# The start of a two-layer decoder step: one hand-ordered list of steps up to the first Strassen tile, activations split straight from PSUM, first weight block on ScalarE's queue

## Chip, cores and metric

One NeuronCore of a Trainium2 chip runs the whole program in one launch. The metric is device time in microseconds (us) per execution, lower is better; the span of the profile is the part of it from the first to the last recorded instruction. TensorE (PE) multiplies, ScalarE (ACT) and VectorE (DVE) do elementwise work, GpSimd (POOL) small things and accumulating DMAs, SyncE (SP) issues most DMAs.

## What is computed

A decoder step for 512 prompt tokens and 8 sample tokens (520 columns in all), width 1024, feed-forward width 2816, two layers. Only the first feed-forward block matters here:

```python
x = x + 0.5 * _swiglu(_rmsnorm(x, norm_g[l, 0]), ffn_w_gate[l, 0], ffn_w_up[l, 0], ffn_w_down[l, 0])

def _swiglu(x, wg, wu, wd):
    return (jax.nn.silu(x @ wg) * (x @ wu)) @ wd
```

Everything is fp32. The kernel reaches that precision with pairs: each operand is split into a high part that TensorE takes exactly and a low part (the rest), and three products (high by high, low by high, high by low) are added.

## The kernel before

**Layout.** Activations are kept turned: eight tiles `x[k]` of 128 rows (128 of the 1024 channels) by 520 tokens. x arrives with tokens in rows, in eight DMAs of 256 KB (`x_load`, L1029: chunk c of 256 channels, in two halves of tokens, called x0.0, x0.1, x1.0, ... below), and is turned on TensorE by transposes (`turn_x`, L1066). The eight sample rows come as two small tiles `xs` on ScalarE's queue (L1018).

**Gate and up product.** The 2816 hidden channels are worked off in 22 tiles of 128. The first three (`NPL[0]`) are plain: two products (gate, up) of 16 parts in all; a part (`part`, L1105, through `mm`, L530) is one k of one product, three terms by two halves of 260 tokens, six matmuls. A product fills a pair of PSUM banks. The later tiles use a Strassen scheme (`strassen_tile`, L629) of seven products of 12 matmuls, for which sums and differences of the x tiles (`sums`, L666) have to be made and split into pairs first. RMSNorm is applied after the products: the row sums of squares are collected in `acc` and turned into `R` by `rstd_tok`, `root` and `rstd_all` (L492 to L524).

**Weights.** `Weights` (L96) loads chunks of 1 MB through SyncE's queue into three rotating buffers and splits them in items of 128 x 512: `hi` on ScalarE (L221, or L195 in the automatic form), the low part on VectorE (L225 or L196). Six split items fit. Items 0 to 3 are the first tile's: gate and up for k 0 to 3 (w0, w1), gate and up for k 4 to 7 (w2, w3). The first chunk comes in four DMAs of 256 KB, issued between the loads of x (L1034 to L1040).

**Order.** A list of steps (`Steps`, L246) carries for each step an engine, a cost, a due time, what it comes after and what buffers it takes; `order` works the list off on paper, on each engine taking the ready step with the earliest due time, and emits the instructions in that order. Each engine then runs its instructions strictly in that order, waiting on semaphores. Lines L1042 to L1182 are such a list for the first tile: t_k (turn x tile k), c_k (copy it to SBUF), s_k (copy its 8 sample columns, L1075), h_k and e_k (high and low part of the scaled x, L1078 and L1082), p_ko (part k of product o), wh_i and wl_i (weight item i), q_k and a_k (square, sum of squares). Its PSUM is three single banks for turned x, one for small things, two pairs for the products. What follows, two plain tiles, the norm, the sums and the first Strassen tile, is written as ordinary code (`ffn`, L689, with `first_hooks`, L1199) and ordered by the automatic scheduler. `begin` (L789) writes the same stretch (plain tiles, norm with a power on GpSimd, sums, products s0 to s5 of the first Strassen tile) as list steps; later feed-forward blocks use it (the fourth at L2392, the second in a similar list behind L1279), the third and the first use the automatic form.

Of the kernel before, what the change touches and what calls it, by code (L numbers as in the profile page):

```python
# [18 lines left out]
P = 128  # L19
D = 1024  # L20
KT = 8
# [295 lines left out]
def yoco_step(ctx, tc, ins, outs):  # L317
# [53 lines left out]
    def ld(dst, src):  # L371
        return lambda raw: later(nc.sync.dma_start(dst(raw), src))
# [8 lines left out]
    def plan_ffn(l, f):  # L381
# [4 lines left out]
        for n in PARTS:  # L386
            for j in range(t0, t0 + n):
# [4 lines left out]
                        ld(lambda raw, k=k, o=o: rows(raw)[:, o, k[0] : k[1], :], w3[:, k[0] : k[1], c])  # L392
# [349 lines left out]
    def weight_steps(st, first, have, count, due, gate=(), width=lambda i: 4, hold=lambda i: []):  # L742
# [16 lines left out]
        for c in sorted(heads):  # L759
# [29 lines left out]
    def begin(st, fi, n, mov, tmp, tt, first, off, base, need, ready, summed, hidden_list, root_):  # L789
# [100 lines left out]
        for p in range(npl):  # L890
# [121 lines left out]
    with ff_pool() as tmp:  # L1012
# [22 lines left out]
        W.begin(2)  # L1035
        x_load(1)
        x_load(2)
        W.begin(4)
# [3 lines left out]
        with tc.tile_pool(name="st", bufs=1, space=bass.MemoryType.PSUM, reuse_waits="tile") as stp:  # L1042
            st = Steps(dict(t=3, m=1, w=6, sq=4))
            add = st.add
            lows, aheads = {}, {}

            def bank(tag, n):
                cnt[0] += 1
                return stp.tile([P, 512], F32, tag=tag, name=f"{tag}{cnt[0]}", bufs=n)

            def warm():
                o = bank("m", 1)
                for _ in range(7):
                    T.matmul(o[:, :P], ones, ones, start=True, stop=True)
# [1377 lines left out]
```

## Time and profile before

| | |
|---|---|
| three runs | 1646.73, 1647.12, 1650.55 us; median 1647.12 |
| the profiled execution | 1648.36 us; its span 1646.6 us |
| TensorE busy | 1633.9 us, 99% of the span |
| VectorE, ScalarE, GpSimd busy | 1237.8, 878.0, 176.8 us |
| mean granted TensorE clock | 0.997 of full speed |

Times of rows are us from the start of the span. A busy TensorE is one with a matmul in flight; how fast it goes is seen from the distance of matmuls and from the granted clock (1.00 is 2.4 GHz, 0.50 is 1.2 GHz). A bracket such as [0.45 <-DMA raw] says how long the engine had been idle before the row and what ended that. In the chain of waits each piece is the work that the next one waited for.

### The profile page before, as it was taken

The numbers are of one execution on the slowest core, as the hardware profiler recorded it, in microseconds if no ns is written. First come the engines' busy times: TensorE is split into PE (matmuls) and PEld (weight loads), VectorE is DVE, ScalarE is ACT, GpSimd is POOL, SyncE is SP. The second block draws the span as 40 slices with busy tenths as digits, with TensorE's granted clock in tenths as the row PEclk, the third lists the DMA queues.
The fourth block names the chain that finished last, engine by engine and source line by source line (L and its number), as shares of the span: only waits on it lengthen the run. The fifth ranks groups of instructions, "written<-read, shape, count | busy, mean of one in ns | idle before, by whom it ended". The sixth has DMA issues, their size and how long they took to land.

```text
span 1646.6 us, 34515 instructions
## 1 busy us (share of the span) xinstructions
PE 1633.9 (99%) x13814; PEld 1620.3 (98%) x13814; DVE 1237.8 (75%) x2341; ACT 878.0 (53%) x1756; POOL 176.8 (11%) x236
## 2 busy tenths in 40 slices
PE   9999999999999999999999999999999999999998
PEld 9999999999999999999999999999989999999998
DVE  7966865878775874878784885778987785785785
ACT  6643643656652652556562552555875663463464
POOL 1101101001101101100201100100220110110100
PEclk9999999999999999999999999999999999999999
DMA  9546846661655755633766666663132575675641
GB/s 245 135 128 129 180 136 140 163 202 54 151 151 135 169 158 135 154 109 97 159 162 154 130 160 159 126 170 103 34 86 71 116 178 141 138 177 137 140 130 53
DMA packets 317567, 226.28 MB, mean 137 GB/s; under 512 B 9536, under 2 KB 293048, under 8 KB 317366
## 3 DMA queue, kind: packets, MB, share of 16 engines
q1 hardware_dynamic: 290976, 178.24, 38.7%
q0 software_dynamic: 23104, 41.31, 15.8%
q10 hardware_dynamic: 3326, 4.53, 0.9%
q8 instruction: 108, 1.77, 0.5%
q14 instruction: 53, 0.43, 0.1%
HBM read 180.63 MB, written 5.04 MB: 113 GB/s over the span
## 4 chain that ended last, share of the span: by engine, by line
PE 95%; DVE 2%; issue 1%; DMA 1%; ACT 0%; SPq 0%; POOLq 0%; POOL 0%; DVEq 0%; ACTq 0%
PE ps L560 48%; PE ps L534 34%; PE pa L534 5%; PE ps L2212 1%; PE pb L1809 1%; PE pc L1880 1%; PE pc L1865 1%; PE p L534 1%; PE ps L1419 1%; DMA pr<-in_bands_dram 1%; PE ps L1382 1%; DMA raw<-in_ffn_w_gate_dram 0%; DVE wl L225 0%; DVE xl L362 0%; DVE acc L487 0%
## 5 line engine op out<-in xcount | busy, mean ns | idle before, releaser
L195 ACT ACTIVATE wh<-raw 128x512 fp32r<-128x512 f32 (+1 forms) x658 | 397.8, 622 | 483.3 <-PE ps L534 284.1
L196 DVE TENSOR_TENSOR wl<-raw,wh 128x512 fp32r<-128x512 f32 (+1 forms) x658 | 435.2, 677 | 175.7 <-ACT wh L195 171.9
L560 PE MATMUL ps<-tl,wh 128*128 128x260 f32 x1248 | 352.4, 282 | 0.0
L560 PE MATMUL ps<-th,wh 128*128 128x260 f32 x1248 | 352.0, 282 | 0.2 <-ACT wh L195 0.2
L560 PE MATMUL ps<-th,wl 128*128 128x260 f32 x1248 | 350.8, 282 | 0.0
L560 PEld LDWEIGHTS ps<-th,wh 128*128 128x128 f32 x1248 | 234.5, 188 | 0.6 <-ACT wh L195 0.4
L560 PEld LDWEIGHTS ps<-tl,wh 128*128 128x128 f32 x1248 | 234.7, 188 | 0.0
L560 PEld LDWEIGHTS ps<-th,wl 128*128 128x128 f32 x1248 | 234.4, 188 | 0.0
L534 PE MATMUL ps<-hl,wh 128*128 128x260 f32 x1024 | 207.2, 282 | 0.0
L534 PE MATMUL ps<-hh,wh 128*128 128x260 f32 x1024 | 206.6, 283 | 0.0
L534 PE MATMUL ps<-hh,wl 128*128 128x260 f32 x1024 | 205.0, 282 | 0.0
L560 PE MATMUL ps<-xh,wh 128*128 128x260 f32 x696 | 195.0, 282 | 0.6 <-ACT sb L643 0.6
L560 PE MATMUL ps<-xl,wh 128*128 128x260 f32 x696 | 194.9, 282 | 0.0
L560 PE MATMUL ps<-xh,wl 128*128 128x260 f32 x696 | 191.6, 282 | 0.0
L158 POOL DMA_DIRECT2D raw<-raw x78 | 69.3, 888 | 1065.0 <-DVE wl L196 387.2
L534 PEld LDWEIGHTS ps<-hl,wh 128*128 128x128 f32 x1024 | 158.3, 188 | 0.0
L534 PEld LDWEIGHTS ps<-hh,wl 128*128 128x128 f32 x1024 | 157.4, 188 | 0.0
L534 PEld LDWEIGHTS ps<-hh,wh 128*128 128x128 f32 x1024 | 157.2, 188 | 0.0
L732 DVE TENSOR_TENSOR u<-ps,R 128x520 f32<-128x520 f32 x86 | 60.0, 698 | 98.5 <-PE ps L534 98.5
L560 PEld LDWEIGHTS ps<-xh,wh 128*128 128x128 f32 x696 | 130.8, 188 | 0.8 <-ACT sb L643 0.8
L560 PEld LDWEIGHTS ps<-xl,wh 128*128 128x128 f32 x696 | 131.1, 188 | 0.0
L534 PE MATMUL ps<-xl,wh 128*128 128x260 f32 x640 | 130.1, 283 | 0.0
(339 smaller groups left out, 3293.3 us busy)
## 6 DMA issues: line engine op xcount, KB each, us to landing
raw<-in_ffn_w_gate_dram SPq DMA_DIRECT2D x87, 512.0 KB
raw<-in_ffn_w_up_dram SPq DMA_DIRECT2D x87, 512.0 KB
raw<-in_ffn_w_down_dram SPq DMA_DIRECT2D x32, 1024.0 KB
S<-in_ffn_w_up_dram SPq DMA_DIRECT2D x78, 256.0 KB
raw<-raw POOLq DMA_DIRECT2D x78, 256.0 KB, 3.3
S<-raw POOLq DMA_DIRECT2D x78, 256.0 KB, 4.5
raw<-in_ffn_w_down_dram SPq DMA_DIRECT2D x16, 768.0 KB
raw<-in_w_q_dram SPq DMA_DIRECT2D x8, 512.0 KB
```

Source lines behind the costliest of these rows:

```text
L158: G.dma_start(blk(raw, 2, 1), blk(raw, 1, 1), accum_op=ALU.add)
L195: nc.scalar.activation(dh, src, AF.Copy)
L196: nc.vector.tensor_tensor(dl, src, dh.bitcast(F32), op=ALU.subtract)
L534: T.matmul(banks[:, hf, :H], a[:, kk, :], hcols(b, hf), start=(first and i == 0), stop=(last and i == 2),)
L560: T.matmul(bank[:, :H], a[:, kk, :], b, start=(not more and kk == 0 and i == 0), stop=(kk == 3 and i == 2), skip_group_check=more,)
L732: V.tensor_tensor(halves(u), banks[m][:, :, :H], halves(R), op=ALU.mult)
L1382: T.matmul(o, a[:, s], b[:, kk, :], start=(n == 0), stop=(n == 5))
L1419: T.matmul(o, za, b, start=(i == 0), stop=(i == len(lst) - 1))
L1809: T.matmul(o, q_[rows_, qc], k_[rows_, kc_], start=(i == 0), stop=(i == 2))
L1865: T.transpose(pt[:, o : o + P], vals["sm", t, h, bi][:, e, kt * P : (kt + 1) * P], ident)
L1880: T.matmul(po[rows_, bi * P : (bi + 1) * P], vtok[:, max(b - 1, 0) + kt, v0 : v0 + 64], vals["pp", t, h, bi][:, kt * 256 + e * P : kt * 25 ...
L2212: T.matmul(bank, a[:, k % 3, :], b[:, c0:c1], start=(k == 0 and i == 0), stop=(k == 5 and i == 2))
```

## The change

The first list now goes on to product s5 of the first Strassen tile, through `begin`, with GpSimd in the order too. x is turned into pairs of PSUM banks (four pairs in all, shared by turned x, both products, the norm and all later tiles), the 8 sample columns are turned in the same step (a fifth transpose), and h_k and e_k read the turned x in PSUM; the copy c_k to SBUF comes after, in one piece, and s_k is gone. A pair is free again when h_k, e_k and c_k have read it. The first weight block (w0) is issued on ScalarE's queue, ahead of the sample rows; w1 to w3 stay on SyncE's. The landing times that the list assumes are new, and so are due times. The square root of the norm is GpSimd's (L808, in `begin`) in place of the twelve small VectorE operations of `root`.

```diff
-    def ld(dst, src):
-        return lambda raw: later(nc.sync.dma_start(dst(raw), src))
+    def ld(dst, src, eng=nc.sync):
+        return lambda raw: later(eng.dma_start(dst(raw), src))
...
+                            lambda raw, k=k, o=o: rows(raw)[:, o, k[0] : k[1], :], w3[:, k[0] : k[1], c],
+                            nc.scalar if k == (0, 4) and o == 0 else nc.sync,
+                        )
                         for k in cuts
                         for o, w3 in ((0, g3), (1, u3))
                     ]
...
-    def weight_steps(st, first, have, count, due, gate=(), width=lambda i: 4, hold=lambda i: []):
...
+            if c in soon:
+                h = heads[c - 2][0]
+                add(f"wa{c}", "POOL", 2.2, due(h) + 0.1, lambda c=c: W.add_up(c), after=[f"wl{h}"])
+                add(f"wd{c}", f"wd{c}", 9.0, -50.0, after=[f"wa{c}"])
+                continue
...
-    def begin(st, fi, n, mov, tmp, tt, first, off, base, need, ready, summed, hidden_list, root_):
...
-        for p in range(npl):
+        for p in range(done, npl):
...
         later(nc.scalar.dma_start(grow, norm_g.rearrange("l n (k p) -> (l n k) p", p=P)))
+        W.begin(1)
         for i in range(2):
...
         x_load(0)
-        W.begin(2)
+        W.begin(1)
         x_load(1)
         x_load(2)
-        W.begin(4)
+        W.begin(2)
         x_load(3)
         W.load(2)
         mov0, tt, st_ = [], {}, {}
-        with tc.tile_pool(name="st", bufs=1, space=bass.MemoryType.PSUM, reuse_waits="tile") as stp:
-            st = Steps(dict(t=3, m=1, w=6, sq=4))
+        open_banks()
+
+        def first_tiles(hs):
+            np_ = NPL[0]
+            st = Steps(dict(d=4, w=6, sb=4, sa=2, g=2, t=2), False)
...
             def turn_g():
-                st_["m"] = o = bank("m", 1)
-                T.transpose(o[:, :48], grow, ident[:48, :48])
-
-            def turn_s():
-                for i in range(KT):
-                    o = st_["m"][:, 64 + i * NS : 64 + (i + 1) * NS]
-                    T.transpose(o, xs[i // 4][:, (i % 4) * P : (i % 4 + 1) * P], ident[:NS, :NS])
+                T.transpose(st_["m"][:, 1, :48], grow, ident[:48, :48])
+
+            def turn_g2():
...
             def turn_x(k):
-                st_["t", k] = pk = bank("t", 3)
+                st_["t", k] = pk = duo().rearrange("p a b -> p (a b)")[:, :TOK]
...
-
-            def copy_x(k, eng, lo, hi):
-                (S.copy if eng == "ACT" else V.tensor_copy)(x[k][:, lo:hi], st_["t", k][:, lo:hi])
-
-            def copy_s(k):
-                V.tensor_copy(x[k][:, SP:TOK], st_["m"][:, 64 + k * NS : 64 + (k + 1) * NS])
+                T.transpose(pk[:, SP:], xs[k // 4][:, (k % 4) * P : (k % 4 + 1) * P], ident[:NS, :NS])
+
+            def copy_x(k, eng):
+                (S.copy if eng == "ACT" else V.tensor_copy)(x[k], st_["t", k])
 
             def x_hi(k):
                 mov0.append(pair(XX, [P, TOK]))
-                S.activation(mov0[k][0], x[k], AF.Copy, scale=gcol(0, k))
+                S.activation(mov0[k][0], st_["t", k], AF.Copy, scale=gcol(0, k))
 
             def x_lo(k):
                 hi, lo = mov0[k]
-                V.scalar_tensor_tensor(lo, x[k], gcol(0, k), hi.bitcast(F32), op0=ALU.mult, op1=ALU.subtract)
+                V.scalar_tensor_tensor(lo, st_["t", k], gcol(0, k), hi.bitcast(F32), op0=ALU.mult, op1=ALU.subtract)
...
-            def w_hi(i):
-                lows[i], aheads[i] = W.hi()
-
-            def w_lo(i):
-                lows.pop(i)()
-                aheads.pop(i)()
-                if i == 4:
-                    W.add_up(3)
...
-                    st_["p", o] = stp.tile([P, 2, 512], F32, tag="p", name=f"p{o}", bufs=2)
+                    st_["p", o] = duo()
...
-            add("i", "POOL", 1.4, -1)
-            add("warm", "PE", 3.0, -1, warm)
-            add("tab", "ACT", 2.4, -1)
-            add("tg", "PE", 0.15, 0, turn_g, after=["i", "lg"])
-            add("cg", "ACT", 0.25, 0.1, lambda: S.copy(gT[:, :48], st_["m"][:, :48]), after=["tg", "tab"])
-            add("ts", "PE", 0.7, 0.2, turn_s, after=["ls", "i", "tg"])
...
+            for name, until in (
+                ("x0.0", 3.7), ("lg", 3.8), ("x0.1", 4.4), ("w0", 4.8), ("ls", 5.0), ("w1", 5.5), ("x1.0", 6.3), ("x1.1", 7.0),
+                ("x2.0", 7.8), ("x2.1", 8.5), ("w2", 9.3), ("w3", 10.0), ("x3.0", 10.8), ("x3.1", 11.5), ("w7", 14.6), ("w11", 17.6),
+            ):
+                land(name, until)
...
+            add("i", "POOL", 3.5, -1)
+            add("warm", "PE", 4.2, -1, warm, takes=("d",))
+            add("tab", "ACT", 4.0, -1)
+            add("tg", "PE", 0.15, 0, turn_g, after=["i", "lg", "warm"], reads=[("g", "preg0")])
+            add("cg", "ACT", 0.22, 0.1, lambda: S.copy(gT[:, :48], st_["m"][:, 1, :48]), after=["tg", "tab"], reads=[("d", "warm")])
...
+            TILE = T0 + 1.6 + UP * 8
+            add("tg2", "PE", 0.12, TILE - 1, turn_g2, after=["i", "t7"], takes=("d",), reads=[("g", "preg1")])
+            add("cg2", "ACT", 0.2, TILE + 6, lambda: S.copy(gT[:, 48:72], st_["m2"][:, :24]), after=["tg2"], reads=[("d", "tg2")])
...
-                    f"t{k}", "PE", 0.45, d, lambda k=k: turn_x(k),
...
-                pieces = [("ACT", 0, 256, 0.37), ("DVE", 256, SP, 0.42)] if k == 0 else [
-                    ("ACT", 0, SP, 0.58) if k % 2 else ("DVE", 0, SP, 0.69)
-                ]
...
-                add(f"s{k}", "DVE", 0.2, d + 0.6, lambda k=k: copy_s(k), after=["ts"])
-                got = [f"c{k}{e[0]}" for e in pieces] + [f"s{k}"]
-                add(f"h{k}", "ACT", 0.72, d + 1, lambda k=k: x_hi(k), after=got + ["cg"] + ([f"h{k - 1}"] if k else []))
-                add(f"e{k}", "DVE", 0.75, d + 1.5, lambda k=k: x_lo(k), after=[f"h{k}"])
+                    f"t{k}", "PE", 0.55, d - 2.4, lambda k=k: turn_x(k),
+                    after=["i", "ls", "tg"] + [f"x{k // 2}.{c}" for c in range(2)] + ([f"t{k - 1}"] if k else []), takes=("d",),
+                )
+                held = [("d", f"t{k}")]
+                add(
+                    f"h{k}", "ACT", 0.72, d + 0.5, lambda k=k: x_hi(k), after=[f"t{k}", "cg"] + ([f"h{k - 1}"] if k else []), reads=held,
+                )
+                add(f"e{k}", "DVE", 0.75, d + 1.0, lambda k=k: x_lo(k), after=[f"h{k}"], reads=held)
+                eng = ("DVE", "ACT")[k % 2]
+                add(
+                    f"c{k}", eng, 0.65 if eng == "ACT" else 0.7, d + 2.0, lambda k=k, eng=eng: copy_x(k, eng), after=[f"t{k}", "tab"] + ([] if k else ["e0"]), reads=held,
+                )
...
-                        f"p{k}{o}", "PE", 0.73, d + 2.3 + 0.7 * o, lambda k=k, o=o: part(k, o),
-                        after=[f"e{k}", f"wl{w}"] + ([f"p{k - 1}{o}"] if k else []),
-                        reads=[("w", f"wh{w}")] if k % 4 == 3 else [],
+                        f"p0.{k}{o}", "PE", 0.73, d + 1.6 + 0.7 * o, lambda k=k, o=o: part(k, o),
+                        after=[f"e{k}", f"wl{w}"] + ([f"p0.{k - 1}{o}"] if k else []),
+                        takes=() if k else ("d",), reads=[("w", f"wh{w}")] if k % 4 == 3 else [],
                     )
...
-                    f"wh{i}", "ACT", 0.63, d, lambda i=i: w_hi(i),
...
-                add(f"o{o}", "ACT", 0.58, T0 + UP * 9 + o, lambda o=o: copy_out(o), after=[f"p7{o}"])
...
+            add("rg", "DVE", 0.7, TILE + 12, gate, after=["o0", "N.c1"])
...
+            def w_due(i):
+                if i < 8:
+                    return (4.6, 5.4, 10.5, 11.2, 17.5, 19.0, 23.0, 24.0)[i]
+                if i < 4 * np_:
+                    return TILE + 2.9 * (i - 4) - 2.0
+                return TILE + 11.6 * (np_ - 1) + 1.4 * (i - 4 * np_) - 5.0
+
+            def landed(i):
+                return [f"w{i}"] if i < 4 else ["w7"] if i < 8 else ["w11"] if i < 12 else []
+
+            weight_steps(st, 0, 0, 4 * np_ + 6 + 4, w_due, hold=landed, soon=(np_,))
+            begin(
+                st, 0, 0, mov0, tmp, tt, 0, 0, TILE - 11.6, lambda k: [], lambda k: [f"c{k}"], ["a7"], lambda: hs, 14.0, 1
+            )
...
-                engines={mybir.EngineType.PE, mybir.EngineType.DVE, mybir.EngineType.Activation}
+                engines={mybir.EngineType.PE, mybir.EngineType.DVE, mybir.EngineType.Activation, mybir.EngineType.Pool}
...
-        open_banks()
-        W.ng = 4
-        there[0] = False
...
-        def first_hooks():
-            steps = sums(tmp, 0, tt)
-            step = lambda: next(steps, None)
...
-                rstd_tok()
-                step()
...
-            def norm_all():
-                rstd_all()
-                known()
...
-            return [step, norm, two, norm_all, two, step, step]
+            begun(0, 0)
...
-        hs0 = ffn(0, tmp, mov0, first_hooks(), tt, HH, deferred(1, tmp, "g", XX, mov1, TW), pool_prep(), first_tile, stop=6)
+        hs0 = ffn(0, tmp, mov0, [], tt, HH, deferred(1, tmp, "g", XX, mov1, TW), pool_prep(), first_tiles, stop=6)
```

## Rows read from the trace of the kernel before

**Rows 1.** The page, busy time of each engine over the span

```profile
PE 1633.9 (99%) x13814; PEld 1620.3 (98%) x13814; DVE 1237.8 (75%) x2341; ACT 878.0 (53%) x1756; POOL 176.8 (11%) x236
```

**Rows 2.** Chain of waits, start and first Strassen tile: start, us, what, matmuls

```profile
9.74 0.85 PE t L1070 x4
10.60 2.36 PE p L534 x18
...
49.40 5.77 PE ps L560 x48
...
56.39 38.89 PE ps L560 x322
```

**Rows 3.** Timeline of the first 8 us, all engines

```profile
1.76 0.47 SPq L372 DMA_DIRECT2D raw<-in_ffn_w_gate_dram  x1
...
4.68 0.20 ACT L1136 COPY gT<-m 128x48 f32<-128x48 f32 x1 [0.95 <-PE m L1059]
5.06 0.20 PEld L1070 LDWEIGHTS t<-ident,xt 128*128 128x128 f32 x2 [0.29 <-DMA xt<-in_x_prompt_dram]
5.43 0.57 PEld L1064 LDWEIGHTS m<-ident,xs 8*128 8x128 f32 x8 [0.17 <-issue]
...
5.95 0.42 DVE L1073 COPY x<-t 128x256 f32<-128x256 f32 x1 [4.92 <-ACT x L1073]
...
6.36 0.63 ACT L221 ACTIVATE wh<-raw 128x512 fp32r<-128x512 f32 x1 [0.45 <-DMA raw<-in_ffn_w_gate_dram]
...
7.66 0.80 PE L534 MATMUL p<-xh,wh 128*128 128x260 f32 x2 [0.98 <-ACT xh L1080]
```

**Rows 4.** DMA view, bytes moved by 4.3, by 5.4 and by 7.8 us

```profile
DMA packets 737, 0.62 MB, mean 143 GB/s; under 512 B 85, under 2 KB 722, under 8 KB 737
...
DMA packets 1392, 0.88 MB, mean 164 GB/s; under 512 B 257, under 2 KB 1376, under 8 KB 1392
...
DMA packets 2482, 1.67 MB, mean 214 GB/s; under 512 B 337, under 2 KB 2466, under 8 KB 2482
```

**Rows 5.** Windows: stretch, length, PE, PEld, DVE, ACT, POOL, PEclk, DMA share, GB/s

```profile
4.00:5.00 1.00, 0.90 (x5) 0.44 (x4) 0.00 (x0) 0.20 (x1) 0.00 (x0) 1.00 0.80 222
7.00:8.00 1.00, 0.34 (x1) 0.34 (x2) 0.98 (x3) 1.00 (x3) 0.00 (x0) 0.75 1.10 358
10.00:11.00 1.00, 1.00 (x7) 1.00 (x6) 1.00 (x2) 0.00 (x0) 0.00 (x0) 0.55 1.15 289
50.00:55.00 5.00, 5.00 (x43) 4.95 (x42) 5.00 (x10) 3.50 (x7) 0.00 (x0) 1.00 0.00 0
```

**Rows 6.** Chain of waits where the second and third feed-forward begin Strassen

```profile
435.52 2.89 PE ps L560 x24
438.42 41.91 PE ps L560 x348
...
802.85 2.90 PE ps L560 x24
806.86 52.12 PE ps L560 x432
```

**Rows 7.** Lines of x's split (source view): count, duration ns min/median/max

```profile
L1080 ACT ACTIVATE xh<-x,gT x8: 712/724/732, 6.9 to 20.0; 128x520 fp32r<-128x520 f32 x8
...
L1084 DVE SCALAR_TENSOR_TENSOR xl<-x,gT,xh x8: 749/756/761, 7.7 to 20.7; 128x520 fp32r<-128x520 f32 x8
...
L1073 DVE COPY x<-t x4: 425/689/692, 5.9 to 16.8; 128x512 f32<-128x512 f32 x3, 128x256 f32<-128x256 f32 x1
```

**Rows 8.** Sample copies, root's first and last operation, GpSimd's power

```profile
L1076 DVE COPY x<-m x8: 155/156/159, 6.3 to 11.4; 128x8 f32<-128x8 f32 x8
...
31.79 0.15 DVE L506 TENSOR_SCALAR nv<-ps 128x5 f32<-128x5 f32 x1
...
35.00 0.16 DVE L513 SCALAR_TENSOR_TENSOR r_tok<-nt,ny 128x5 f32<-128x5 f32 x1
...
L809 POOL TENSOR_TENSOR r_tok<-nv,minus_half x2: 1247/1655/2063, 409.4 to 1286.3; 128x5 f32<-128x5 f32 x2
```

More of the change, by code (lines that the diff above doesn't have):

```diff
@@ L740, in ffn, with weight_steps @@
         return hs
-    def weight_steps(st, first, have, count, due, gate=(), width=lambda i: 4, hold=lambda i: []):
+    def weight_steps(st, first, have, count, due, gate=(), width=lambda i: 4, hold=lambda i: [], soon=()):
         add = st.add
@@ L787, in weight_steps, with begin @@
             add(f"wl{i}", "DVE", 0.14 * n + 0.13, due(i), lambda i=i: w_lo(i), after=[f"wh{i}"] + ([f"wl{i - 1}"] if i else []))
-    def begin(st, fi, n, mov, tmp, tt, first, off, base, need, ready, summed, hidden_list, root_):
+    def begin(st, fi, n, mov, tmp, tt, first, off, base, need, ready, summed, hidden_list, root_, done=0):
         add, vals = st.add, {}
@@ L1112, in copy_out @@
                 S.copy(halves(z), st_["p", o][:, :, :H])
-            def land(name, cost):
-                add(name, "DMA", cost, len(st.steps) - 1000)
-            land("l", 2.4)
-            land("lg", 0.1)
-            for c in range(2):
-                land(f"x0.{c}", 0.87)
-            land("ls", 0.1)
-            for o in range(2):
-                land(f"w{o}", 0.87)
-            for c in range(2, 6):
-                land(f"x{c // 2}.{c % 2}", 0.87)
-            for o in range(2, 4):
-                land(f"w{o}", 0.87)
@@ new lines, in silu, with times, land @@
+            def silu():
+                g = st_["o", 0]
+                S.activation(g, g, AF.Silu)
+            def times():
+                g, t = (st_["o", o] for o in range(2))
+                V.scalar_tensor_tensor(g, t, -1.0, g, op0=ALU.mult, op1=ALU.mult)
+            at_ = [0.0]
+            def land(name, until):
+                add(name, "DMA", until - at_[0], len(st.steps) - 1000)
+                at_[0] = until
+            for name, until in (
[3 more added lines that the diff above has]
+                land(name, until)
@@ L1163, in yoco_step @@
                     )
                 late = d + 9
-                add(f"q{k}", "ACT", 0.63, late, lambda k=k: x_square(k), after=got + [f"h{min(k + 3, 7)}"], takes=("sq",))
+                add(f"q{k}", "ACT", 0.63, late, lambda k=k: x_square(k), after=[f"c{k}", f"h{min(k + 4, 7)}"] + ([f"q{k - 1}"] if k else []), takes=("sb",))
                 add(
                     f"a{k}", "DVE", 0.69, late + 0.5, lambda k=k: x_sum(k),
-                    after=[f"q{k}"] + ([f"a{k - 1}"] if k else []), reads=[("sq", f"q{k}")],
+                    after=[f"q{k}"] + ([f"a{k - 1}"] if k else []), reads=[("sb", f"q{k}")],
@@ new lines, in first_tiles @@
+            add("rg", "DVE", 0.7, TILE + 12, gate, after=["o0", "N.c1"])
+            add("rs", "ACT", 0.65, TILE + 12.3, silu, after=["rg"])
+            add("rm", "DVE", 0.7, TILE + 12.6, times, after=["rs", "o1"], reads=[("t", "o1")])
+            add("Hh0", "ACT", 0.65, TILE + 14, lambda: hidden(st_["o", 0], hs, 0), after=["rm"])
+            add("Hl0", "DVE", 0.7, TILE + 14.5, lambda: hidden_lo(st_["o", 0], hs[0]), after=["Hh0"], reads=[("g", "o0")])
+            def w_due(i):
[4 more added lines that the diff above has]
+                return TILE + 11.6 * (np_ - 1) + 1.4 * (i - 4 * np_) - 5.0
@@ L1181, in yoco_step @@
             ):
                 st.emit()
-        open_banks()
-        W.ng = 4
-        there[0] = False
-        def first_tile(hs):
-            g, t = (st_["o", o] for o in range(2))
-            def rest():
-                V.tensor_tensor(g, g, R, op=ALU.mult)
-                S.activation(g, g, AF.Silu)
-                V.scalar_tensor_tensor(g, t, -1.0, g, op0=ALU.mult, op1=ALU.mult)
-                hidden(g, hs)
-            copied.append(rest)
-            return 1
-        def first_hooks():
-            steps = sums(tmp, 0, tt)
-            step = lambda: next(steps, None)
-            def norm():
-                pg = ps()
-                T.transpose(pg[:, :24], grow2, ident[:24, :24])
-                S.copy(gT[:, 48:72], pg[:, :24])
-                rstd_tok()
-                step()
-            def norm_all():
-                rstd_all()
-                known()
-            def two():
-                step()
-                step()
-            return [step, norm, two, norm_all, two, step, step]
+            begun(0, 0)
@@ L1220, in yoco_step @@
+            return np_ + 1
         prep = {}
```

35 lines of the change are left out of this document (13 added, 22 removed).

## Prediction, made before the change was run

> **What bounds the kernel now.** The page comes first: TensorE is busy 1633.9 of 1646.6 us [rows 1], so 12.7 us of idle in the whole program are all that an order can win, apart from work done at half clock. The chain of waits says where the start loses. Products begin at 7.66 us, after 0.98 us of idle that the high part of x ended [rows 3]; the first part of the first product and the transposes of the third x tile are over at 10.60 [rows 2]. From there TensorE is the chain without a break until the first Strassen tile, which runs four products from 49.40 to 55.17 (49.40 + 5.77) and goes on at 56.39: 1.22 us lost [rows 2]. VectorE is busy in all of the five us before that [rows 5]. The granted clock is 1.00 in the us from 4, 0.75 in the us from 7 and 0.55 in the us from 10 [rows 5]: it fell to 1.2 GHz at about 7.5, when TensorE was idle, and was back at 2.4 GHz at about 10.9. So the change can win at three places: when products start, how long they run slow, and the 1.22 us.
>
> **Start: x, and a new wait.** Before, high part h_0 stood behind two things on ScalarE: the copy of x and the split of w0, which began at 6.36 after waiting 0.45 us for its DMA [rows 3]. The change takes the copies out of the way and lets h_0 read PSUM. But it also changes TensorE's order. Work its list off with its own figures: second half of x1 landed at 7.0 (so t_2 is ready at 7.1), the pair of banks free (t_0, t_1 and t_2 hold three of four), and the first part p_00 ready only at about 7.6, after e_0. So t_2 is emitted ahead of p_00; before it came after it. TensorE then waits for x1 with the whole product stream queued behind it. When does x1 land? By bytes: x0 is 0.52 MB and the small loads 0.09; 0.62 MB were moved at 4.3 us and TensorE's wait for the second half of x0 ended at 5.06. With w0 it is 0.87 MB, moved at 5.4, and ScalarE's wait for w0 ended at 6.36 [rows 3, 4]. So landing follows the last byte by 0.75 to 1.0 us. x0, w0, w1, x1 and the small loads are 1.66 MB, moved at 7.8 [rows 4]: x1 lands at 8.55 to 8.8, I take 8.65, not 7.0. Then t_2's last two transposes at the slow clock (0.43, half of the 0.85 of [rows 2]), the sample transpose (0.57 / 8 = 0.07 [rows 3], 0.14 slow), and p_00 at half speed: 18 matmuls in 2.36 [rows 2] are 0.13 each with a slow first stretch, four full-speed products of 12 in 5.77 are 0.12 each; six at half clock 1.44. That ends at 10.66, against 10.60 for the same work before: **+0.06**. Here goes the gain of the earlier split: h_0 and e_0 are done by about 8 (x0, w0 and the samples behind it land by 6.4, then 0.72 and 0.76 [rows 7]), and what is late next is x1. Bounds: if x1 lands as the list says, p_00 is over at 8.8, and the rest of the slow stretch costs 1.05: 0.9 earlier than now. If the clock comes back 2 us later because TensorE is idle from 6.7 to 7.9, it costs 1.0 more.
>
> The Trainium skill, DMA: Bandwidth & Descriptors, section Issuing engines are not separate DMA queues, speaks against w0 on ScalarE's queue: transfers from several engines share the same DMA engines, and only issue time is saved. The trace has a DMA share of 0.80 at 222 GB/s from 4 to 5 us and 1.10 at 358 from 7 to 8 [rows 5], so there is a hole of some 0.1 MB that a second queue might fill; by that x1 would land 0.25 us sooner, by the page not at all. I take the bytes as they flowed, and leave the 0.25 to the early bound.
>
> **Issues moved.** w0 leaves SyncE's queue (0.47 us of issue) and goes ahead of xs and the activation table on ScalarE. ScalarE had been idle 0.95 us before its first use, the copy of gT, which waited for TensorE [rows 3]; that cover is twice the cost. If it were gone, 0.5 us would show only in h_0, which has the slack until x1. SyncE's later loads go up by one issue.
>
> **Sample columns.** The eight transposes (0.57 together) ran in TensorE's idle time before the first product; now five of them, of t_3 to t_7, lie in the stream: 5 x 0.07 = **+0.35**. The eight copies s_k leave VectorE, 8 x 0.16 [rows 8].
>
> **Norm.** Twelve small VectorE operations between 31.79 and 35.16 [rows 8] go, about 2 us of VectorE; GpSimd's power takes 1.25 to 2.06. TensorE's share is the same. If the sums come as now, the power starts at 31.94 and ends by 34.0, 1.2 before root ends now, at which the products did not stop. On GpSimd it is queued behind the accumulating DMAs of chunk 3 (wa3 is now early in the list), which wait for that chunk; the 1.2 us are the cover. Cost nothing; with the cover gone, R comes late, the gate tiles hold pairs of banks, and TensorE would wait in the third tile.
>
> **First Strassen tile.** The same stretch stands three more times in the program; two of them are shown. In list form there is no gap: 435.52 + 2.89 = 438.41, next at 438.42. In automatic form 802.85 + 2.90 = 805.75, next at 806.86: 1.11 lost [rows 6]. So the form goes with the loss, and VectorE, which was full before it, is relieved of some 3 us (8 x 0.16 and about 2). I take the whole gap: **-1.22**; bounds -1.22 and 0.
>
> **Sum.** 0.06 + 0.35 - 1.22 = -0.81 us. Against the profiled execution, 1648.36, that is 1647.6; against the median, 1647.12, which I forecast, **1646.3 us**. The two differ by 1.24, more than the sum; a measurement of this kernel tells about 0.3% (4.9 us) from no change.
>
> **Rivals.**
> *Early start.* x1 lands near 7, as the list assumes. For it: the hole in the DMA share. Against it: 1.66 MB at 7.8. Then -0.9 + 0.35 - 1.22 = -1.8, 1645.3; if besides the clock never falls, p_00 is over at 8.1 at full speed, 2.5 earlier, and with the five sample transposes and the gap the sum is -3.4, 1643.7.
>
> *The gap stays.* The split of weights into six buffers sets the pace, not VectorE, and the first Strassen tile waits as before or its successor does. For it: ScalarE's splits ended the waits there. Against: the list form elsewhere. Then +0.41, 1647.5.
>
> *Pairs held too long, slower.* Each t_k holds a pair until three readers are through, and only two pairs rotate once the products have theirs. Now three single banks had one reader each. The readers do not overlap: when both engines copied halves of one bank, VectorE's copy began at 5.95, when ScalarE's had ended [rows 3]. The Trainium skill, PSUM — Partial Sum Buffer, section PSUM bank collisions raise a hardware error, says that any two engines on one bank must be kept apart, reads too; the row agrees. A hold is 0.5 (transposes), 0.72, 0.76 and 0.69 [rows 7], 2.67 us, and TensorE needs 1.94 per tile (12 matmuls of 0.12 and 0.5), so it decides from a hold of 3.88. Two foreign operations, as long as 0.72 and 0.76, ahead of the readers on each engine make 5.63, 0.88 per tile too much, for six tiles 5.3: 1651.6; three make 7.11, 9.7 us, 1656.0; middle 1653.8. For it: ScalarE has splits, copies and squares queued between. Against it: they come later by due time.
>
> *The automatic rest shifts.* What follows the list is ordered anew; a new stall is of the size of the 1.11 at 805.75, either way.
>
> **Chances.** Forecast 0.50, early start 0.23, gap stays 0.12, pairs held 0.08, automatic rest 0.07. Low end 1643.6: the early start with the clock kept. High end 1649.3: the forecast with the late clock (+1.0), the gap kept (+1.22), and a run as much above its median as the profiled one was (some 1). Left out are the held pairs and the far ends, under 2 in 10. Faster by over 0.3% (below 1642.2) needs the far early end and a lucky rest, 0.05; slower (above 1652.1) needs held pairs in their upper half or a stall of another kind, 0.06; within, 0.89.
>
> **What the profile would show.** Right: TensorE idle before t_2 with the DMA of x as releaser, t_2's end near 9.2, a fall of the clock about 7.5, the first tile's end 0 to 1 us later than now, no gap at the first Strassen product's successors. Wrong: products before 7.5, TensorE waiting for a copy of x in the first tile (held pairs), a wait for ScalarE's split near 55, or a difference of over 2 us that arises after 60 us.

## The result and the profile after

The changed kernel takes **1650.76 us** (median of 22 runs, 1648.09 to 1653.47); 22 runs of the kernel before beside it took 1648.28 (1646.73 to 1650.55). The ratio is **1.0016** [1.0011, 1.0022]: 2.6 us slower, below the 0.3% that the prediction called distinguishable, but clear of 1 with this many runs, outside the stated range and of the other sign. The forecast was 4.5 us lower; 1.2 of that is its base, a median of three runs (1647.12). The profiled execution took 1650.75 us, its span is 1649.0, 2.4 more than before.

The page, busy time of each engine over the span of the changed kernel:

```profile
PE 1636.5 (99%) x13814; PEld 1621.7 (98%) x13814; DVE 1235.5 (75%) x2322; ACT 876.5 (53%) x1755; POOL 180.6 (11%) x237
```

It answers to [rows 1]: TensorE does as many instructions, 2.6 us longer. Idle time is about what it was (12.5 us for 12.7), so what was lost lies mostly within TensorE's busy time. The chain of waits of the changed kernel, start and first Strassen tile (start, us, what, matmuls; L1075 turns a block of x, L1076 the samples):

```profile
1.24 5.48 DMA xt<-in_x_prompt_dram
...
6.77 0.69 PE ps L1075 x2
...
10.15 2.90 PE ps L537 x12
13.05 0.46 PE ps L1075 x4
13.51 0.15 PE ps L1076
13.66 1.64 PE ps L537 x12
15.30 0.44 PE ps L1075 x4
15.74 0.15 PE ps L1076
...
22.56 4.50 PE ps L537 x36
27.07 0.17 PE ps L1069
...
52.72 16.31 PE ps L563 x134
...
69.04 28.75 PE ps L563 x238
97.79 0.48 PE ps L537 x4
```

The same chain before, behind the pieces of [rows 2]:

```profile
12.96 0.87 PE t L1070 x8
13.84 1.44 PE p L534 x12
...
16.59 7.20 PE p L534 x60
...
95.28 0.48 PE ps L534 x4
```

Cut at four points that both kernels pass, this places the difference as far as 98 us:

| point reached | before | after | lost in the stretch |
|---|---|---|---|
| five x tiles turned, 24 product matmuls done | 13.84 | 15.89 | +2.05 |
| first tile done (96 matmuls) | 23.79 | 27.07 | +1.23 |
| first Strassen product | 49.40 | 52.72 | +0.04 |
| a chain row some four Strassen tiles on (L534 x4, L537 x4) | 95.28 | 97.79 | -0.81 |
| end of the span | 1646.6 | 1649.0 | -0.11 |

The gap of 1.22 at the first Strassen tile is gone; of it 0.81 arrives at the fourth point. The rest was not placed: the list has 372 matmuls in that stretch for 370 before, 0.24 at 0.12 each. The losses up to there are all at the start: 2.05 until the fifth tile, and 1.23 while t_5 to t_7 are turned in the stream.

The -0.11 of the last stretch is small only because larger differences cancel in it. In the chains of waits of before and then of the changed kernel, two places read:

```profile
375.56 10.00 PE ps L1382 x84
...
1212.29 1.46 PE pb L1809 x12
```

```profile
378.37 11.57 PE ps L1364 x84
...
1216.12 0.90 PE pb L1791 x12
```

Both are stretches of low clock in one profile and not in the other. The changed kernel's granted clock was 0.55 from 378 to 380 and 0.60 from 380 to 382, which cost 1.57; that of the kernel before was 0.50 from 1213 to 1215, and what it ran from 1212.29 to 1216.11, 3.82, takes the changed kernel 2.29, a cost of 1.53. The group of 84 took 10.0 us in six of the fourteen profiles of this document and 11.4 to 11.6 in eight, among these run 2, in which only w0 was moved. So one pair of profiles can't tell a difference of this size behind the start; the ratios of many runs can.

The second loss is visible on TensorE's weight loads. Timeline of the changed kernel, engine PEld:

```profile
13.44 0.13 PEld L1076 LDWEIGHTS ps<-ident,xs 8*128 8x128 f32 x1 [0.17 <-issue]
13.59 0.30 PEld L537 LDWEIGHTS ps<-xh,wh 128*128 128x128 f32 x2
...
15.03 0.47 PEld L1075 LDWEIGHTS ps<-ident,xt 128*128 128x128 f32 x4
15.67 0.13 PEld L1076 LDWEIGHTS ps<-ident,xs 8*128 8x128 f32 x1 [0.17 <-issue]
```

Loads otherwise run ahead of the matmuls before them: the one at 15.03 begins before the product at 14.90 is through. The load for an 8-row sample transpose starts only 0.17 after the last load ended (0.33 in the slow stretch at 7.4 to 9.9), and the product's load behind it follows only when it is done. The source view of the line adds it up:

```profile
L1076 PEld LDWEIGHTS ps<-ident,xs x8: 133/134/178, 7.4 to 22.3; 8*128 8x128 f32 x8
...
  issue: 1.8, 8
```

Eight times, 1.8 us. The same bracket stands in [rows 3], at 5.43, once for eight transposes in a row. The few columns of the result are not what does it: in the same profile two matmuls of 8 columns (L825, timeline and source view), but with 128 rows in their load, stand in the stream with no idle time ahead of it.

```profile
37.07 0.30 PEld L825 LDWEIGHTS ps<-ident,r_tok 128*128 128x128 f32 x2
...
L825 PE MATMUL ps<-ident,r_tok x6: 175/216/256, 37.2 to 1291.7; 128*128 128x8 f32 x6
```

### The profile page after: what moved, and what is told of

It reads as the page before. It is cut to its first block, busy times and chain, and to the rows that moved or that the text cites. A ratio compares the mean times of both kernels' runs of the same rounds, so it can differ in the third digit from the quotient of the medians.

```text
span 1649.0 us, 34502 instructions
## 1 busy us (share of the span) xinstructions
PE 1636.5 (99%) x13814; PEld 1621.7 (98%) x13814; DVE 1235.5 (75%) x2322; ACT 876.5 (53%) x1755; POOL 180.6 (11%) x237
## 4 chain that ended last, share of the span: by engine, by line
PE 94%; DVE 2%; DMA 1%; issue 1%; ACT 1%; POOLq 0%; POOL 0%; SPq 0%; DVEq 0%; ACTq 0%
PE ps L563 47%; PE ps L537 35%; PE pa L537 5%; PE ps L2194 1%; PE pb L1791 1%; PE pc L1862 1%; PE pc L1847 1%; PE ps L1401 1%; DMA pr<-in_bands_dram 1%; PE ps L1364 1%; DMA xt<-in_x_prompt_dram 0%; PE ps L1075 0%; DMA pr<-in_pool_w_dram 0%; DVE xl L362 0%; DVE sm L1810 0%
## 5 line engine op out<-in xcount | busy, mean ns | idle before, releaser
L195 ACT ACTIVATE wh<-raw 128x512 fp32r<-128x512 f32 (+1 forms) x646 | 389.9, 621 | 471.4 <-PE ps L537 276.0
L196 DVE TENSOR_TENSOR wl<-raw,wh 128x512 fp32r<-128x512 f32 (+1 forms) x646 | 426.6, 677 | 173.2 <-ACT wh L195 169.5
L537 PE MATMUL ps<-hl,wh 128*128 128x260 f32 x1024 | 207.1, 282 | 0.0
L537 PE MATMUL ps<-hh,wh 128*128 128x260 f32 x1024 | 206.7, 283 | 0.0
L537 PE MATMUL ps<-hh,wl 128*128 128x260 f32 x1024 | 205.0, 282 | 0.0
L563 PE MATMUL ps<-xh,wh 128*128 128x260 f32 x696 | 195.3, 283 | 0.0
L563 PE MATMUL ps<-xl,wh 128*128 128x260 f32 x696 | 194.9, 282 | 0.0
L563 PE MATMUL ps<-xh,wl 128*128 128x260 f32 x696 | 191.9, 282 | 0.0
L537 PEld LDWEIGHTS ps<-hl,wh 128*128 128x128 f32 x1024 | 158.2, 188 | 0.0
L537 PEld LDWEIGHTS ps<-hh,wl 128*128 128x128 f32 x1024 | 157.3, 188 | 0.0
L537 PEld LDWEIGHTS ps<-hh,wh 128*128 128x128 f32 x1024 | 157.2, 188 | 0.0
L537 PE MATMUL ps<-xh,wh 128*128 128x260 f32 x672 | 137.4, 286 | 0.0
L537 PE MATMUL ps<-xl,wh 128*128 128x260 f32 x672 | 136.9, 284 | 0.0
L537 PE MATMUL ps<-xh,wl 128*128 128x260 f32 x672 | 135.5, 283 | 0.0
```

The costliest lines, as they stand in the source:

```text
L195: nc.scalar.activation(dh, src, AF.Copy)
L196: nc.vector.tensor_tensor(dl, src, dh.bitcast(F32), op=ALU.subtract)
L537: T.matmul(banks[:, hf, :H], a[:, kk, :], hcols(b, hf), start=(first and i == 0), stop=(last and i == 2),)
L563: T.matmul(bank[:, :H], a[:, kk, :], b, start=(not more and kk == 0 and i == 0), stop=(kk == 3 and i == 2), skip_group_check=more,)
```

## The experiments

The theories after the first profile: **S**, the sample transposes in the stream cost more than their length; **L**, w0 on ScalarE's queue delays x0; **O**, the list's order (t_2 ahead of the first product) holds the products back; **X**, only the samples behind w0 on that queue are late; **W**, weights further on take back what the start gains. Each run's kernel does the whole computation. Ratios are to the kernel before on the same chip; traces are of one execution each.

### 1. w0 back on SyncE's queue

```diff
-                            nc.scalar if k == (0, 4) and o == 0 else nc.sync,
+                            nc.sync,
...
         later(nc.scalar.dma_start(grow, norm_g.rearrange("l n (k p) -> (l n k) p", p=P)))
-        W.begin(1)
...
         x_load(0)
-        W.begin(1)
+        W.begin(2)
```

> The changed kernel with w0 back on SyncE's queue, behind x0; the list with its orders stays. Theory L (w0 on ScalarE's queue shares the DMA engines with x0 and makes its second half land at 6.73 instead of 5.05): x0 lands near 5.05 again; t_2 then waits for x1, which lands near 8.65, so the first product starts near 9.3 instead of 10.08, 0.8 us earlier, and the kernel is 0.8 us faster than the changed one (about 1.7 us slower than the kernel before). Theory S (the eight sample transposes inside the stream cost the time, about 0.35 us each): first product earlier, but the five later ones still cost 1.75 in the first tile, so 1.5 us or more of the 2.5 stay. If L were all of it, the kernel would come down by the whole 2.5.

Measured: 1651.07 us, 1.0007 [0.9997, 1.0017]. x0 was on time, but t_2 now waited for x1. TensorE in the timeline of this run:

```profile
8.15 0.44 PE L1074 MATMUL ps<-ident,xt 128*128 128x128 f32 x2 [1.18 <-DMA xt<-in_x_prompt_dram]
...
8.90 0.44 PE L1074 MATMUL ps<-ident,xt 128*128 128x128 f32 x2 [0.32 <-DMA xt<-in_x_prompt_dram]
...
9.43 0.51 PE L537 MATMUL ps<-xh,wh 128*128 128x260 f32 x2
```

That is the wait that the prediction worked out (x1 at 8.55 to 8.8). The first Strassen product is at 52.25: only 0.47 of the 3.32 came back in this profile, so theory L explains little of it.

### 2. The kernel before with w0 on ScalarE's queue

```diff
+                            nc.scalar if k == (0, 4) and o == 0 else nc.sync,
...
+        W.begin(1)
         for i in range(2):
             later(nc.scalar.dma_start(xs[i], x_sample[:, 0, i * 512 : (i + 1) * 512]))
```

> The kernel before with w0 on ScalarE's queue ahead of the sample rows, nothing else. Theory L: the second half of x0 lands near 6.7, the first product moves from 7.66 to about 9.2, the kernel gets 1 to 1.5 us slower. Theory S alone: w0 lands a little earlier (6.18 against 6.36), x is late but the split of w0 was what the first product waited for, so no change (within 0.5 us).

Measured: 1650.0 us, 1.0006 [0.9996, 1.0016]. The chain of waits of this run:

```profile
2.46 4.85 DMA xs<-in_x_sample_dram
...
8.85 2.03 PE p L537 x6
...
51.84 5.77 PE ps L563 x48
```

x0 was on time (all four of its transposes ran from 4.75), so it was not x0 that was delayed. Two loads of 16 KB behind 256 KB on one queue took 4.85 us; the first product came at 8.85 instead of 7.66, Strassen at 51.84 instead of 49.40. Of these 2.44, 1.36 is slow clock: 18 matmuls take 3.72 here for 2.36 in [rows 2], at a granted clock of 0.50 from 9 to 15. In this order, where everything waits for the samples, the queue costs in this profile; the ratio's interval still holds 1.

### 3. Sample transposes of 128 rows

The sample tiles get 128 rows, 120 of them zero, so that the fifth transpose has the shape of the other four.

```diff
-        xs = [big.tile([NS, 512], F32, tag=t, name="xs") for t in HH]
+        xs = [big.tile([P, 512], F32, tag=t, name="xs") for t in HH]
+        for z in xs:
+            V.memset(z, 0.0)
...
-                T.transpose(pk[:, SP:], xs[k // 4][:, (k % 4) * P : (k % 4 + 1) * P], ident[:NS, :NS])
+                T.transpose(pk[:, SP : SP + P], xs[k // 4][:, (k % 4) * P : (k % 4 + 1) * P], ident)
```

> The changed kernel with the sample rows laid in tiles of 128 rows (the rest zero), so that their transposes have the shape of the others, 128 x 128; nothing else. Theory S (the 8-row transpose makes TensorE wait 0.17 us before it and about as much after it): each one costs 0.11 instead of 0.35, no idle time in front of it, the first tile shrinks by 5 x 0.24 = 1.2 us, and 0.5 to 0.9 more in the slow stretch: 1.2 to 2.0 us faster than the changed kernel. Theory L alone, or a cost of switching between transposes and products whatever their shape: no change, or 0.04 x 8 = 0.3 us slower.

Measured: 1648.43 us, 0.9999 [0.9990, 1.0007]. The chain of waits of this run (L1079 is the sample transpose):

```profile
14.76 0.44 PE ps L1078 x4
15.20 0.11 PE ps L1079
15.31 1.45 PE ps L537 x12
...
21.28 4.31 PE ps L537 x36
```

Twelve product matmuls take 1.45 where they took 1.64, 36 take 4.31 for 4.50, and the transpose is 0.11 for 0.15; weights now load ahead, with no idle time at full clock. Per tile 0.23 of chain is saved. Theory S holds: a transpose of sixteen times the rows is the cheaper one.

### 4. w0 on SyncE's queue, and landing times of the kernel before

```diff
-                ("x0.0", 3.7), ("lg", 3.8), ("x0.1", 4.4), ("w0", 4.8), ("ls", 5.0), ("w1", 5.5), ("x1.0", 6.3), ("x1.1", 7.0),
+                ("lg", 4.2), ("x0.0", 4.4), ("ls", 4.9), ("x0.1", 5.0), ("w0", 6.3), ("w1", 7.2), ("x1.0", 8.0), ("x1.1", 8.7),
```

(The later entries likewise; beside the edit of run 1.) The list then puts the first part of the first product ahead of t_2.

> The changed kernel with w0 on SyncE's queue and with landing times in the list as the trace of the kernel before shows them (x0 5.0, w0 6.3, w1 7.2, x1 8.7, ...), by which the first part of the first product comes ahead of t_2. Theory L with the order: first product near 7.3, 2.7 us earlier than in the changed kernel, of which some goes at the slow clock; 1.5 to 2 us faster than the changed kernel, 0.5 to 1 slower than the kernel before for the samples in the stream. Theory S alone: 0 to 0.5 us faster than the changed kernel.

Measured: 1650.23 us, 1.0006 [0.9995, 1.0017], so in time no better than run 1, although Strassen began at 50.02, 2.2 earlier, and TensorE ran at full speed from 5.8 on. The chain of waits of this run says what ended last after that:

```profile
50.02 14.87 PE ps L563 x122
...
69.99 7.64 DMA raw<-in_ffn_w_up_dram
...
78.75 8.61 DMA S<-raw
...
96.36 0.53 PE ps L537 x4
```

From 65 to 93 the chain is not TensorE but weights: a load, an accumulating DMA of 8.61, splits on ScalarE and VectorE. Of 2.70 us gained on the changed kernel at 50, 1.43 are left at the last row (96.36 for 97.79).

### 5. The changed kernel once more

No edit.

> The changed kernel itself once more, on the chip of the three that follow. Both theories: 2 to 3 us slower than the kernel before; x0's second half lands at 6.5 to 6.9, the first product starts at 9.8 to 10.3. If the end of the slow stretch at 13.2 was an accident of that one profile, it ends elsewhere here and the first tile's end moves by half of that.

Measured: 1651.83 us, 1.0020 [1.0012, 1.0029]. The timeline of this run:

```profile
5.61 0.63 ACT L221 ACTIVATE wh<-raw 128x512 fp32r<-128x512 f32 x1 [0.70 <-DMA raw<-in_ffn_w_gate_dram]
...
5.83 0.18 PEld L1076 LDWEIGHTS ps<-ident,xs 8*128 8x128 f32 x1 [0.51 <-DMA xs<-in_x_sample_dram]
...
8.00 1.50 PE L1075 MATMUL ps<-ident,xt 128*128 128x128 f32 x4 [0.65 <-DMA xt<-in_x_prompt_dram]
```

x0 was there at 4.6, so its late half in the first profile (6.77) was that execution's; no other profile with w0 on ScalarE's queue (runs 2, 3, 6, 10, 11) has it. Here w0 did come earlier, 5.61 for 6.36 [rows 3], and its low part was done at 6.95, but the products were queued behind t_2 and x1: the first at 9.62, Strassen at 52.68, as late as in the first profile. The slow stretch ended near 13.5, for 13.2 there, so it was no accident of that one profile.

### 6. Samples ahead of w0 on ScalarE's queue

```diff
-        W.begin(1)
         for i in range(2):
             later(nc.scalar.dma_start(xs[i], x_sample[:, 0, i * 512 : (i + 1) * 512]))
+        W.begin(1)
```

> The changed kernel with the sample rows issued ahead of w0 on ScalarE's queue (w0 goes out about 0.9 us later). Theory L as first stated (w0 takes its share from x0): x0's second half still lands after 6, at 6.2 to 6.7, first product at 9.5 to 10.2, within 0.5 us of the changed kernel. Theory X (what is late is the sample rows, behind 256 KB of w0 on their own queue; in the kernel before with w0 moved, TensorE waited for them until 7.3): the rows are there by 5, the first tile's transposes end 0.3 to 0.6 us earlier only if x0 is not the later one.

Measured: 1653.91 us, 1.0026 [1.0017, 1.0035]: the slowest of all. w0 fell back instead, and x1 with it. Timeline of this run:

```profile
8.63 0.63 ACT L221 ACTIVATE wh<-raw 128x512 fp32r<-128x512 f32 x1 [3.82 <-DMA raw<-in_ffn_w_gate_dram]
...
8.88 1.41 PE L1075 MATMUL ps<-ident,xt 128*128 128x128 f32 x4 [2.65 <-DMA xt<-in_x_prompt_dram]
```

The samples did come early, as theory X would have it (their first transpose, at 5.27, waited for no load; in run 5 it waited until 5.83). It won nothing: what was late then was w0 and x1.

### 7 and 8. Runs 3 and 4 together, twice

The edits of runs 3 and 4 in one kernel, measured twice.

> All three start costs undone in the changed kernel: w0 on SyncE's queue, true landing times, sample transposes of 128 rows. Theories L and S together: first product near 7.4, the first Strassen product at 48.7 to 49.2 (50.02 without the wide transposes), no gap behind it; if nothing else limits, 1.5 us faster than the kernel before. Theory W (a chain that the start does not change, weights loaded, summed by DMA and split, ends last in the tiles after the first Strassen tile, as TensorE's late stretch between 65 and 93 us with the true landing times suggests): the end of the first eight tiles stays near 96, and the kernel is level with the kernel before, within 0.7 us.

> The kernel of the run with all three costs of the start undone (first weights on SyncE's queue, landing times and order of the kernel before, 128-row sample transposes), unchanged, for a second measurement. If the three costs are what made the change slower and the closed gap is a real gain, the ratio to the kernel before is below 1 again, 0.9985 to 0.9995 (0.8 to 2.5 us faster), first product by 7.8, no gap after the first Strassen products. If the first measurement was chance, 1.0000 or above.

Measured: 1647.29 us, 0.9991 [0.9983, 1.0000], and 1647.09 us, 0.9993 [0.9984, 1.0002]. The chain of waits of the first of the two:

```profile
49.16 16.34 PE ps L563 x134
...
94.44 0.50 PE ps L537 x4
```

No gap, and the last row at 94.44 (95.07 in the second) for 95.28 before. The ratios put them 1.3 us below the kernel before on average, about what the gap alone would give (1.22). Each interval reaches 1, so the gain over the kernel before is likely, not certain; that over the changed kernel (0.9992 for 1.0016 to 1.0020) is clear.

### 9. Runs 1 and 3 together

w0 on SyncE's queue and 128-row sample transposes, the list's own order.

> The changed kernel with the first weights back on SyncE's queue and with 128-row sample transposes, but with its own landing times and order (third x tile turned ahead of the first product). If queue and sample transposes add up as they measured alone (0.0010 and 0.0018 of 1.0017), this comes out at 0.9988 to 0.9995 of the kernel before, and the order of the list is worth nothing. If the wait for the second x chunk with all products behind it is itself a cost of about 1 us, it comes out near 0.9997 to 1.0003, above the run with the order of the kernel before by 0.0006.

Measured: 1649.69 us, 1.0002 [0.9993, 1.0011]; the first product at 9.25, Strassen at 51.19, against 49.16 and 49.94 with the order of runs 7 and 8. Windows of this run (columns as in [rows 5]) show what the late start costs:

```profile
7.00:8.00 1.00, 0.00 (x0) 0.00 (x0) 0.24 (x1) 0.90 (x2) 0.00 (x0) 1.00 1.09 365
...
12.00:13.00 1.00, 1.00 (x7) 1.00 (x6) 0.87 (x2) 0.00 (x0) 0.00 (x0) 0.50 1.05 338
```

TensorE stands idle through the us from 7, and is still at 1.2 GHz in the us from 12; in the kernel before it was back at 2.4 at about 10.9. With the order of the kernel before eighteen matmuls took 2.17 from 10.57 in run 7 and 2.16 from 11.35 in run 8, 0.12 each, which is full speed; in run 8 the granted clock was 0.50 from 8 to 10 and 0.52 in the us from 10.

### 10 and 11. Only the landing times changed

The changed kernel with w0 still on ScalarE's queue and later landing times in the list ("w0" 6.1, "x1.1" 9.0), once with 8-row and once with 128-row sample transposes.

> The changed kernel, first weights on ScalarE's queue and 8-row sample transposes kept; only the landing times that the list assumes are later, so that the first product's first part stands ahead of the third x tile. If the order (all products behind a transpose that waits for the second x chunk) is what the start loses, the first Strassen product moves from 52.7 to about 50.5 and the ratio from 1.0018 to 1.0005 to 1.0010; if the queue is what counts, products still wait for x or the sample rows, Strassen stays near 52 and the ratio near 1.0015.

> The same with 128-row sample transposes: all of the change but its order and its 8-row transposes. If the queue costs nothing of its own, this is as fast as the run with the first weights on SyncE (0.9985 to 0.9997, first Strassen product near 49.5) or faster by the earlier split of the first weights (5.6 against 7.1); if the queue costs 1 us of its own, 0.9997 to 1.0003, Strassen near 50.5 to 51.

Measured: 1651.09 us, 1.0011 [1.0002, 1.0020], and 1649.9 us, 0.9999 [0.9990, 1.0008]. These landing times didn't do what they were meant to: the list still put t_2 first (in run 10 the first product is at 9.29, Strassen at 52.18; in run 11 at 8.90 and 50.02), so order and queue were not told apart this way. As a pair they tell the sample transposes' cost again, 0.0012.

### 12. The old start, a second list for the gap alone

The first list is that of the kernel before; a second one, through `begin`, orders the two plain tiles, the norm and the first Strassen tile.

```diff
+        def first_tiles(hs):
+            np_ = NPL[0]
+            st = Steps(dict(d=4, w=6, sb=4, sa=2, g=2, t=2), False)
...
+            weight_steps(st, 0, 8, 4 * np_ + 6 + 4, w_due)
...
+            begin(st, 0, 0, mov0, tmp, tt, 0, 0, -11.6, lambda k: [], lambda k: [], ["all"], lambda: hs, 14.0, 1)
```

> The start of the kernel before, list and PSUM unchanged, and then a second list by begin for the two plain tiles, the norm and the first Strassen tile, as in the changed kernel (undoes the start, keeps the rest of the change). Theories L and S: first product at 7.7, first tile's end at 23.8 as before, the norm's root on GpSimd, first Strassen product at 49.4, and no gap: 1.2 us faster than the kernel before. Theory W: the gap at 55 is gone but the same 1.2 us come back as a wait before 100: within 0.4 us of the kernel before.

Measured: 1650.98 us, 1.0005 [0.9995, 1.0015], a miss: it was to show the gap's worth alone and does not. The chain of waits of this run:

```profile
24.69 0.60 ACT t L1112
...
55.55 0.65 ACT wh L221
...
56.96 9.11 PE ps L560 x72
```

The seam between the lists waits for a copy out of PSUM (0.65), and the first Strassen tile for a weight split (1.69 with what stands ahead of it), which I put down to the due times of my list: the gap moved rather than went. Its first product also came late, at 8.54, because w0's split could begin only at 7.24 in this execution (6.36 before, with the same start).

## Why the prediction was wrong

**Taken together.** With nothing else changed, 128-row instead of 8-row sample transposes lower the ratio in four pairs: from 1.0016 or 1.0020 to 0.9999 (run 3), 1.0007 to 1.0002 (runs 1, 9), 1.0006 to 0.9992 (runs 4, 7 and 8), 1.0011 to 0.9999 (runs 10, 11). The mean is 0.0012 to 0.0013, 2.1 us. Each ratio's interval reaches 0.0005 to 0.0011 to either side, so that only the first pair and perhaps the third are clear of noise by themselves; the mean of four, by an estimate from these intervals, is good to some 1 us. Queue and order of the kernel before, put back together, lower the ratio by 0.0012 with 8-row transposes (1.0018 to 1.0006) and by 0.0007 with 128-row ones (0.9999 to 0.9992): about 1.6 us, less certain, though in the traces the first Strassen product moves with it (52.7 to 50.0, and 51.2 to 49.2 and 49.9). What is left with both undone, -1.3, I take for the gap, which the traces of runs 7 and 8 no longer have; run 12, meant to show it alone, did not. 2.1 + 1.6 - 1.3 = +2.4, for 2.6 and 3.3 measured; the parts come from the same ratios as the whole, so that they add up proves little.

**Sample columns, +0.35: the step that failed.** I took the length of eight transposes in a row, divided by eight. That row's own bracket [rows 3] had the price: 0.17 of idle ahead of the group. Spread over the stream it is paid at each transpose (0.15 of chain in all), and again by the product behind it: 12 matmuls take 1.64 for 1.45. That is 0.34 each, 1.7 for the five in the stream, five times the term; the 1.23 of the table is three transposes and four such products. In time, padding all eight to 128 rows won about 2.1 us. The Trainium skill, TensorEngine Tiling (Array Packing), section Key Properties, says that a change of tiling mode drains TensorE; the rows agree with a drain at each change of row count (1.8 us of idle in eight), though no run here shows which mode the 8-row transpose runs in. The Trainium skill, TensorE: Matmul & The Clock Gate, section Step-by-step: what each phase is for, says that the row count doesn't matter for a load's time. The load alone agrees, 133 ns with 8 rows and 139 at the least with 128 (run 3); what stands around it does not.

**Start, +0.06: the second step that failed.** Its mechanism was right: t_2 ahead of p_00, TensorE waiting for x1 with the products behind it, x1 at 8.8 to 9.0 (runs 1, 5, 9), and the earlier w0 (run 5) worth nothing. Only in the first profile was it x0's second half, at 6.77, that TensorE waited for. The first product began at 9.62 in run 5, for 9.22 by the prediction's working (8.65 + 0.43 + 0.14). The size was not right: 2.05 until the fifth tile, of which the sample transposes of t_3 and t_4 and the product between them are 0.49, so the start's own is near 1.6. I let the clock come back at 10.9 as before and kept "2 us later, 1.0 more" as a bound. That bound was the case: in the changed kernel the first twelve matmuls take 2.90 for 1.44 at full clock, 1.46 more, and pairs stand 0.43 apart until 12.85. But the reason that I gave for it, TensorE idle from 6.7 to 7.9, was not the one in the first profile. There the clock was low before the wait, though the granted clock reads 1.00 (see the last section); two loads of the first transposes, before and after, from the timelines:

```profile
4.57 0.20 PEld L1070 LDWEIGHTS t<-ident,xt 128*128 128x128 f32 x2
...
4.60 0.29 PEld L1075 LDWEIGHTS ps<-ident,xt 128*128 128x128 f32 x2
```

0.29 is what the next two take at 6.76 too, and the matmul pairs 0.43 apart follow. In run 1 the clock was back for the transposes of 8.15 (0.20 a pair) and low again from 10 to 13 (0.50), after the us from 7 without work. What lowers it at 4.6 was not tried. The runs put the order and the queue together at 1.6 us; run 2 shows the queue delaying the samples, run 9 the order delaying the products, and by how much each counts alone in the changed kernel stays open: undone singly the queue is worth 0.0011 with 8-row transposes and nothing (0.9999 to 1.0002) with 128-row ones.

**Issues moved, at nothing.** ScalarE's cover held: its idle time before the copy of gT shrank from 0.95 to 0.48 and was not used up. The samples behind w0, by the prediction landed by 6.4, let TensorE go on at 5.8 in run 5, but only at 7.35 in run 2.

**First Strassen tile, -1.22: right in what it does.** No gap in any run of the one list (1, 3 to 11); in the first profile 0.81 of it was left at 98 us, and in time runs 7 and 8 are 1.3 faster than before. Theory W is what can eat it: in runs 1, 4, 5, 6, 11 and 12 weights ended last between 70 and 96, not in the others. Where they did, the slowest accumulating DMA there took 7.9 to 8.6, in the others 5.2 to 8.0; 5.9 in the first profile and 8.5 in run 5, the same kernel. So it comes and goes between executions of one kernel; that the slow DMA is its cause is likely from the chains and not shown, as the two ranges touch.

**Norm, VectorE: right.** VectorE is 2.3 us less busy [rows 1], for some 3 forecast, and no wait of TensorE in the first 100 us is for the norm or for GpSimd.

**Rivals.** No early start: where TensorE waited for x1, its second half came at 8.3 (run 11) to 9.6 (run 6), not near 7. No held pairs: no TensorE wait in the first tile on a copy of x. The gap did not stay, though in the six runs of theory W a later tile waits instead, as that rival allowed. The automatic rest showed no new stall that one of the two kernels alone would have: 1.57 at 378 us and 1.53 back at 1212 are clock. None of the four had the two losses that count: the shape of a 0.07 us transpose and the long slow clock. The high end's own terms (1646.3 + 1.0 + 1.22 + 1) add up to 1649.5, not 1649.3; with the price in [rows 3] (0.17 idle by 8, 1.36) the slower side would have reached 1650.9, just past the result.

## What to carry to other kernels

When small matrix operations are moved from a group into a stream, cost each by the idle bracket ahead of the group plus what the work behind it loses, not by the group's mean; padding them to the shape of their neighbours can be the cheaper form. An order that puts a transfer's consumer ahead of products that could be ready sooner can cost twice, by the wait and by the clock that is low behind it (run 9: an idle us, then 0.50 from 10 to 13). Landing times that a list assumes should be those that the trace shows. And a difference between two single profiles is the change's only if it stays when the clock row of both is beside it.

## What the runs showed of the hardware

An 8-row transpose between 128-row work costs 0.17 of idle ahead of its weight load at full clock, 0.33 at half, and the next product's load does not run ahead of it; a 128-row one (run 3), 0.11 at full clock, costs neither.

The profile's clock row can miss a slow stretch. In the changed kernel's window the granted clock reads 1.00, while its timeline has matmul pairs 0.43 apart, twice the 0.24 of the same pairs at 14.18 to 14.90:

```profile
11.00:12.00 1.00, 1.00 (x7) 1.00 (x7) 1.00 (x3) 0.49 (x1) 0.00 (x0) 1.00 1.02 289
```

Seven matmul records in that us, as in the half-clock us of [rows 5] (x7 from 10, at 0.55); run 5 has seven at a reading of 1.00 there too. So: count the records, or their distance, beside the clock row.

With the same start, w0's split began at 6.36 in one execution and at 7.24 in another, and the changed kernel waited 1.48 for x0 in its first profile and not at all in run 5. One profile of a start is one sample of its landings; ratios over many runs decide.
